# Attention's logits and values as full-array products, the other head's half filled with zeros

## The chip, the core and the metric

The kernel runs on one core of one Trainium2 chip. The metric is the device time of one execution in microseconds (us), the median of several runs; less is better. TensorE (PE) does the matrix products and has a row of its own for its weight loads (PEld); VectorE (DVE), ScalarE (ACT) and GpSimd (POOL) do the rest, and SyncE (SP) issues the transfers.

## The reference

Two transformer blocks over 256 tokens of width 1024, in float32. Block 1 adds a mixer of three branches and an MLP; block 2 has two layers, each a mixer and an MLP. What matters here are the attentions, 40 heads of width 64 in all:

- block 1: 8 query heads over 2 key heads, on the 64 keys per query that an index score picks (4 index heads of width 64), with a learned bias;
- block 2, layer 0: 8 heads with forget gates and 8 heads with a relative bias;
- block 2, layer 1: 8 stick-breaking heads and 8 latent heads, whose queries and keys have 96 rows (64 plain, 32 rotary).

```python
s = jnp.einsum('bqhd,bkhd->bhqk', qb, k).astype(jnp.float32) * scale   # logits
...
p = jax.nn.softmax(jnp.where(mask, s, -jnp.inf), axis=-1)
return jnp.einsum('bhqk,bkhd->bqhd', p.astype(v.dtype), v)             # values
```

Around them stand dense products with weights: 1024 to some 6,700 columns in block 1's mixer, 1024 to 4096 and back in each of the three MLPs.

## The kernel before

Activations lie transposed: features on the 128 partitions, the 256 tokens along the free axis, in K tiles of 128 features. All weights are one stream of 128 by 128 blocks in the order of use. A unit of eight blocks is split into two parts, `whi` on ACT (L168) and `wlo` on DVE (L170), five units in flight of each. A dense product takes three products of parts per block: L225, L228, L229 where features stay on partitions, L264 (`gemm_tokens`) where tokens come out on partitions, as the attention's values do; L237 and L238 are the wide form of the MLP's second product.

Attention is side work. `pipeline` is a generator over the heads; `slot`, called after each dense tile, runs its next step, and the step's instructions are put among the dense ones. A planner that simulates the engines in time settles the order on each queue. A step has the logits of one head (`scores`, L409 and L416) with its softmax (L427 to L433), the transposes of an earlier head's weights (`transpose_p`, L439), and the values product of the head before that (`pv`, L446 and L447), after whose second head ACT and DVE split the pair's result (`split`, L271 and L272).

Two heads share a 128-row tile: head g of a pair lies in rows 64g to 64g+63 of `qT` and `kT`. Logits of one head are taken from those 64 rows alone, a 64 by 128 form of the array; in block 1 and layer 0 the second query block goes in three products of parts (`kh`, `kl`, `qh`, `ql`). Values of one head take 64 columns of the values as the loaded operand, a 128 by 64 form, and write 64 partitions of the bank `po`; the pair's other head writes the other 64. Latent heads take 96 rows. Three small products use few rows: index weights (L535, 4 rows), the forget gates' sums per query (L877, 8 rows) and per key (L914, 40 rows). A float32 product stands in the trace as two matmul records, a product of parts as one.

The queries come from L898 (layer 0) and L990 (layer 1), one DVE instruction of 128 by 256 that applies the norm's scale; the values from `gemm_tokens`, evicted by ACT at L267. The linear attention's products at L722 use 32 and 64 columns, and its last products, L743 and L744, are float32 of 128 by 128 with the same moving widths as L446 and L447.

Of the kernel before, what the change touches and what calls it, by code (L numbers as in the profile page):

```python
# [18 lines left out]
T = 256  # L19
# [56 lines left out]
def kernel(  # L76
# [47 lines left out]
    # the first products want the first K tiles of both operands  # L124
# [11 lines left out]
    nc.vector.memset(eps, EPS)  # L136
    ident = cst[:, C_ID:C_ID + 128]
# [83 lines left out]
    def gemm(ps, ks, ah, al, prev=None):  # L221
        """ps = W.T @ a over the K tiles ks; three of the four products of the parts."""
# [9 lines left out]
    def gemm_wide(kt, a):  # L232
        """[128, 2, T] of which the halves' sum is W.T @ a, both parts of a[:, k] at once."""
# [22 lines left out]
    def gemm_tokens(kt, ah, al, dst, scale=None, steps=1):  # L256
        """dst(b) [128, 256] = (a.T @ W)[128 * b:] for 256 columns of W, times scale[:, b]: tokens on partitions."""
# [8 lines left out]
        for b, ps in enumerate(banks):  # L266
            nc.scalar.activation(out=dst(b), in_=ps, func=AF.Copy, scale=1.0 if scale is None else scale[:, b:b + 1])  # L267
# [6 lines left out]
    def rsqrt(src, n, inv_n, dst, room=None):  # L274
        """dst = (src * inv_n + EPS) ** -0.5 over [128, n]: exp(-ln/2) and a Newton step."""
# [8 lines left out]
    def softplus_neg_abs(dst, z):  # L284
        """dst = ln(1 + exp(-|z|))"""
# [4 lines left out]
    def sigmoid(dst, z, t):  # L290
        """dst = exp(min(z, 0) - ln(1 + exp(-|z|)))"""
# [5 lines left out]
    def operand(j, gain):  # L297
        """Operand parts of x[:, j] * gain."""
# [6 lines left out]
    def squares(j):  # L305
        """The squares of x[:, j] on top of those before."""
# [22 lines left out]
    def rstd_tokens():  # L329
        """rtok[t, b] = rstd of token 128 * b + t"""  # L330
# [20 lines left out]
    def mlp(gain_next):  # L351
# [6 lines left out]
        with ExitStack() as st:  # L358
# [11 lines left out]
            for j in range(KD):  # L370
                # the sum of the parts costs a step, which the last tile does without
# [5 lines left out]
                # the last tile of all goes on in halves of the tokens  # L377
# [18 lines left out]
    def v_natural(dst, vT, rows):  # L396
        """dst[:, kt, :] = vT[:, kt * 128:].T"""
        ps = pt_p.tile([128, 512], FP32, name="pt")
        n = rows.stop - rows.start
        for kt in range(2):  # L400
            nc.tensor.transpose(out=ps[:, kt * n:(kt + 1) * n], in_=vT[rows, kt * 128:(kt + 1) * 128],
                                identity=ident[rows, rows])
        src = ps[:, 0:2 * n].rearrange("p (k c) -> p k c", k=2)
        nc.scalar.activation(out=dst, in_=src, func=AF.Copy)

    def scores(qT, kT, rows, parts=None):
# [37 lines left out]
    def pv(po, pT, v, cols):  # L444
        """po [64, 256] = (P @ v).T: keys 0..127 for all queries, keys 128..255 for queries 128..255."""
        m = nc.tensor.matmul(out=po, lhsT=v[:, 0, cols], rhs=pT[:, 0:256], start=True, stop=False)  # L446
        after(nc.tensor.matmul(out=po[:, 128:256], lhsT=v[:, 1, cols], rhs=pT[:, 256:384], start=False, stop=True), m)  # L447

    class Pair:
        """Two heads whose outputs fill one K tile of the next product: probs(g) gives [128, 384] of weights,  # L450
        v the values, oh and ol the parts to fill."""
# [11 lines left out]
        def s3(self, g):  # L463
            if g == 0:
                self.po = po_p.tile([128, 512], FP32, name="po")[:, 0:T]
            v = self.v() if callable(self.v) else self.v
            pv(self.po[g * HD:(g + 1) * HD], self.pT.pop(g), v, slice(g * HD, (g + 1) * HD))
# [7 lines left out]
    def pipeline(pairs, d):  # L475
        """The heads of the pairs one step apart: logits and softmax, d steps later transposes, then values."""
# [14 lines left out]
    # ================= block 1 =================  # L491
# [16 lines left out]
    with ExitStack() as st:  # L508
# [13 lines left out]
        # -- sparse attention: index queries and keys, then keys, values and queries --  # L522
        ps = gemm1(KD, xh, xl)
        ikT = att.tile([128, T], FP32, name="ikT")
        nc.vector.tensor_tensor(out=ikT[0:64], in0=ps[0:64], in1=rstd[0:64], op=ALU.mult)
        nc.vector.tensor_tensor(out=ikT[64:128], in0=ps[0:64], in1=rstd[0:64], op=ALU.mult)
        iwT = att.tile([128, 384], FP32, name="ir", bufs=2)[:, 0:T]
        nc.vector.scalar_tensor_tensor(out=iwT[64:68], in0=ps[64:68], scalar=1.0 / 16.0, in1=rstd[64:68],
                                       op0=ALU.mult, op1=ALU.mult)
        iw = att.tile([128, 2, 4], FP32, name="iw")  # L530

        def index_weights():
            ps = pt_p.tile([128, 512], FP32, name="pt")
            for b in range(2):
                nc.tensor.transpose(out=ps[:, b * 4:b * 4 + 4], in_=iwT[64:68, b * 128:(b + 1) * 128],  # L535
                                    identity=ident[64:68, 64:68])
# [11 lines left out]
        vn = att.tile([128, 2, 128], FP32, name="vn")  # L548

        def select():  # L550
            """Index scores (block 0 in columns 0..127, block 1 in 128..383) and what they leave out."""
            for h in range(4):
                rows = slice(64 * (h % 2), 64 * (h % 2) + 64)
                ps = scores(iqT[:, h // 2], ikT, rows)
# [734 lines left out]
```

## Time and profile before

| | us |
|---|---|
| median of 3 runs | 1100.3 (1099.16 to 1103.56) |
| span of the profiled execution | 1098.2 |
| PE busy | 1078.4 (98%) |
| DVE busy | 833.4 (76%) |
| ACT busy | 600.9 (55%) |
| POOL busy | 151.2 (14%) |

The profile is of one execution on the one core; its granted TensorE clock was full nearly throughout (mean 0.998). In time order the span holds: block 1's mixer to about 290 us (attention's index scores from 20, its heads from 77 to 123, linear attention to 200, gates and output to 290), MLP to 468, layer 0's mixer to 610 (attention 485 to 605), MLP to 786, layer 1's mixer to 918 (attention 798 to 910), MLP and last norm to 1098. A matmul's record lasts from its start to the modelled end of its pipeline, so records overlap; how fast PE works is read from start to start.

### The profile page before, as it was taken

What the parts mean: (1) busy time and instruction counts of PE and PEld (TensorE: products, weight loads), DVE (VectorE), ACT (ScalarE), POOL (GpSimd) and SP (SyncE); (2) the same over time, 40 slices, a digit from 0 to 9 for tenths busy, and PEclk for the clock granted to TensorE, in tenths of its full rate; (3) what the DMA queues carried; (4) which work ended last, traced back from release to release, by engine and by line L of the source; (5) the groups of instructions that cost most, each with busy time, mean ns of one, the idle gap of its engine ahead of it and who ended that gap; (6) DMA issues with size and microseconds to landing.
All of it is one profiled execution on the core that took longest, in us unless ns stands there. A gap on an engine that the chain in (4) does not pass through costs nothing. (4 is left out here: it accounts for less than half of the span.)

```text
span 1098.2 us, 20294 instructions
## 1 busy us (share of the span) xinstructions
PE 1078.4 (98%) x8132; PEld 1008.0 (92%) x8132; DVE 833.4 (76%) x1606; ACT 600.9 (55%) x943; POOL 151.2 (14%) x164
## 2 busy tenths in 40 slices
PE   7999999999999999999999999999999999999996
PEld 6998989999999988998888999988999889999886
DVE  7999798887986666687667866666689679776663
ACT  6467456665565544455554555444458655555441
POOL 1035450110300001110001200011021004000110
PEclk9999999999999999999999999999999999999999
DMA  8543333454455554563333545455454323555541
GB/s 308 201 164 135 127 144 132 181 192 155 169 216 192 192 179 179 184 226 116 116 116 116 191 179 181 182 189 192 154 192 154 116 93 142 209 195 195 186 174 39
DMA packets 29007, 183.94 MB, mean 167 GB/s; under 512 B 3056, under 2 KB 6384, under 8 KB 7280
## 3 DMA queue, kind: packets, MB, share of 16 engines
q1 hardware_dynamic: 28768, 182.50, 45.7%
q8 instruction: 64, 1.05, 0.4%
q14 instruction: 31, 0.25, 0.1%
q10 hardware_dynamic: 144, 0.13, 0.0%
HBM read 181.57 MB, written 1.05 MB: 166 GB/s over the span
## 5 line engine op out<-in xcount | busy, mean ns | idle before, releaser
L170 DVE TENSOR_TENSOR wlo<-stg,whi 128x512 fp32r<-128x512 f32 (+1 forms) x676 | 473.3, 741 | 164.9 <-ACT whi L168 160.8
L168 ACT ACTIVATE whi<-stg 128x1024 fp32r<-128x1024 f32 (+1 forms) x340 | 356.2, 1051 | 343.7 <-PE pg L228 195.7
L225 PE MATMUL pg<-xh,whi 128*128 128x256 f32 x1472 | 416.0, 283 | 7.2 <-ACT whi L168 6.8
L229 PE MATMUL pg<-xh,wlo 128*128 128x256 f32 x1472 | 414.1, 282 | 0.6 <-DVE wlo L170 0.6
L228 PE MATMUL pg<-xl,whi 128*128 128x256 f32 x1472 | 413.3, 281 | 0.6 <-DVE xl L300 0.6
L225 PEld LDWEIGHTS pg<-xh,whi 128*128 128x128 f32 x1472 | 277.4, 189 | 12.6 <-ACT whi L168 7.1
L229 PEld LDWEIGHTS pg<-xh,wlo 128*128 128x128 f32 x1472 | 279.4, 190 | 2.7 <-DVE wlo L170 1.3
L228 PEld LDWEIGHTS pg<-xl,whi 128*128 128x128 f32 x1472 | 277.9, 189 | 3.3 <-issue 1.2
L237 PE MATMUL pg<-hid,whi 128*128 128x512 f32 x672 | 236.1, 396 | 0.0
L238 PE MATMUL pg<-hid,wlo 128*128 128x256 f32 x672 | 188.5, 281 | 0.0
L237 PEld LDWEIGHTS pg<-hid,whi 128*128 128x128 f32 x672 | 126.1, 188 | 30.1
L238 PEld LDWEIGHTS pg<-hid,wlo 128*128 128x128 f32 x672 | 127.0, 189 | 0.0
L308 POOL TENSOR_TENSOR sqa<-xv 128x256 f32<-128x256 f32 x6 | 4.3, 720 | 480.3 <-DVE xv L384 300.1
L312 POOL TENSOR_TENSOR sq<-xv 128x256 f32<-128x256 f32 x36 | 27.7, 776 | 175.6 <-DVE xv L384 171.7
L429 ACT ACTIVATE p<-p,m 128x128 f32<-128x128 f32 x64 | 28.5, 446 | 23.1 <-DVE m L427 22.8
L228 PE MATMUL pg<-ol,whi 128*128 128x256 f32 x128 | 37.1, 292 | 0.0
L264 PE MATMUL pg<-whi,xh 128*128 128x256 f32 x128 | 37.1, 290 | 0.0
L313 POOL TENSOR_TENSOR sqa<-sqa,sq 128x256 f32<-128x256 f32 x36 | 36.7, 1019 | 2.4
L225 PE MATMUL pg<-oh,whi 128*128 128x256 f32 x128 | 36.0, 291 | 0.5 <-ACT oh L271 0.5
L229 PE MATMUL pg<-oh,wlo 128*128 128x256 f32 x128 | 36.2, 285 | 0.0
L369 DVE TENSOR_TENSOR hid<-s,hid 128x512 fp32r<-128x512 f32 x48 | 33.1, 690 | 4.0
L264 PE MATMUL pg<-wlo,xh 128*128 128x256 f32 x128 | 35.9, 281 | 0.0
(344 smaller groups left out, 1565.1 us busy)
## 6 DMA issues: line engine op xcount, KB each, us to landing
stg<-w SPq DMA_DIRECT2D x168, 1024.0 KB, 4.8
t<-t_bias SPq DMA_DIRECT2D x8, 128.0 KB, 2.8
cb<-chk_bias SPq DMA_DIRECT2D x1, 1024.0 KB, 4.7
xv<-x_in SPq DMA_DIRECT2D x2, 384.0 KB, 6.1
cst<-consts SPq DMA_DIRECT2D x1, 640.0 KB, 10.9
stg<-w SPq DMA_DIRECT2D x1, 512.0 KB, 7.8
out<-xg SPq DMA_DIRECT2D x2, 256.0 KB, 2.5
stg<-w SPq DMA_DIRECT2D x1, 384.0 KB, 6.5
```

Source lines behind the costliest of these rows:

```text
L168: act = [nc.scalar.activation(out=h[:, z], in_=src[:, z], func=AF.Copy) for z in (pieces if u == 0 else [slice(0, UW)])]
L170: dve = [nc.vector.tensor_tensor(out=l[:, z], in0=src[:, z], in1=h[:, z], op=ALU.subtract) for z in pieces]
L225: m0 = nc.tensor.matmul(out=ps, lhsT=h, rhs=ah[:, k], start=(k == ks[0]), stop=False)
L228: nc.tensor.matmul(out=ps, lhsT=h, rhs=al[:, k], start=False, stop=False)
L229: m1 = nc.tensor.matmul(out=ps, lhsT=l, rhs=ah[:, k], start=False, stop=(k == ks[-1]))
L237: nc.tensor.matmul(out=ps, lhsT=h, rhs=a[:, k], start=(k == 0), stop=False)
L238: nc.tensor.matmul(out=ps[:, 1], lhsT=l, rhs=a[:, k, 0], start=False, stop=(k == kt - 1))
L264: nc.tensor.matmul(out=ps, lhsT=a[:, k, t], rhs=w_, start=(k == 0 and i == 0), stop=(k == kt - 1 and i == 2))
L312: nc.gpsimd.tensor_tensor(out=s, in0=x[:, j], in1=x[:, j], op=ALU.mult)
L313: nc.gpsimd.tensor_tensor(out=sqa, in0=sqa, in1=s, op=ALU.add)
L369: nc.vector.tensor_tensor(out=hid[:, j:j + 2, 1], in0=s, in1=hid[:, j:j + 2, 0], op=ALU.subtract)
L429: nc.scalar.activation(out=p[:, a:b], in_=p[:, a:b], func=AF.Exp, scale=-1.0, bias=m[:, i:i + 1], accum_out=sums[:, i:i + 1])
```

## The change

Every product of attention takes all 128 rows and all 128 columns of the array. Where two heads share a tile, one operand gets a copy per head, `[128, 2, ...]`, in which the other head's 64 rows are zero, so a product over 128 rows gives one head's logits. For block 1 that operand is the keys (`ikT`, `kz` and its parts), for the other two the queries (`qT`, `qh`, `ql`), made by one DVE instruction of twice the width against a scale `rq` that is zero in the other half. Values stand in a tile with 64 zero columns after each head's 64 (`values_room`, zeroed once by POOL), so that 128 columns taken at the right place hold one head's values in its half and zeros in the other; both heads of a pair then add into all of `po`, as one group of four products. The 4-, 8- and 40-row products get 128 rows. Latent heads' logits keep 96 rows, and L722 is not touched. To make room, some tiles share buffers: `isc` takes one of the three of `p`, `bm` those of `ir`, `kz` that of `ikT`, and the squares and scales of the two latents one each.

The diff, cut to its core (the same edits recur where "..." stands):

```diff
+    half = keep.tile([128, 2], FP32, name="half")
+    nc.gpsimd.memset(half, 0.0)
+    for g in range(2):
+        nc.gpsimd.memset(half[64 * g:64 * g + 64, g:g + 1], HD ** -0.5)
...
+    def values_room(name, heads):
+        v = att.tile([128, 2, heads, 128], FP32, name=name)
+        nc.gpsimd.memset(v[:, :, :, 64:128], 0.0)
+        return v
+    def head_values(v, h):
+        o = 128 * h - 64 * (h % 2)
+        return [v[:, kt].rearrange("p h c -> p (h c)")[:, o:o + 128] for kt in range(2)]
...
-        nc.tensor.matmul(out=ps[:, 0:128], lhsT=qT[rows, 0:128], rhs=kT[rows, 0:128], start=True, stop=True)
+        nc.tensor.matmul(out=ps[:, 0:128], lhsT=qT[:, 0:128], rhs=kT[:, 0:128], start=True, stop=True)
...
-            nc.tensor.matmul(out=ps[:, 128:384], lhsT=q[rows], rhs=k[rows, 0:256], start=(i == 0), stop=(i == len(terms) - 1))
+            nc.tensor.matmul(out=ps[:, 128:384], lhsT=q, rhs=k[:, 0:256], start=(i == 0), stop=(i == len(terms) - 1))
...
+    def query_scale(name):
+        r = att.tile([128, 2, T], FP32, name=name)
+        for g in range(2):
+            nc.vector.tensor_scalar(out=r[:, g], in0=rstd, scalar1=half[:, g:g + 1], scalar2=None, op0=ALU.mult)
+        return r
...
-    def pv(po, pT, v, cols):
-        m = nc.tensor.matmul(out=po, lhsT=v[:, 0, cols], rhs=pT[:, 0:256], start=True, stop=False)
-        after(nc.tensor.matmul(out=po[:, 128:256], lhsT=v[:, 1, cols], rhs=pT[:, 256:384], start=False, stop=True), m)
+    def pv(po, pT, v, g):
+        m = nc.tensor.matmul(out=po, lhsT=v[0], rhs=pT[:, 0:256], start=(g == 0), stop=False)
+        after(nc.tensor.matmul(out=po[:, 128:256], lhsT=v[1], rhs=pT[:, 256:384], start=False, stop=(g == 1)), m)
...
-            pv(self.po[g * HD:(g + 1) * HD], self.pT.pop(g), v, slice(g * HD, (g + 1) * HD))
+            pv(self.po, self.pT.pop(g), self.v(g), g)
...
+        ikT = att.tile([128, 2, T], FP32, name="ikT")
+        nc.gpsimd.memset(ikT[64:128, 0], 0.0)
+        nc.gpsimd.memset(ikT[0:64, 1], 0.0)
...
-        isc = att.tile([128, 384], FP32, name="isc")
+        isc = att.tile([128, 384], FP32, name="p", bufs=pb["p"])
...
+                made["kz"] = kz = att.tile([128, 2, T], FP32, name="ikT")
+                for g in range(2):
+                    nc.vector.scalar_tensor_tensor(out=kz[:, g], in0=raw[:, 0], scalar=gk[:, g:g + 1], in1=rr[:, 0:T],
+                                                   op0=ALU.mult, op1=ALU.mult)
...
-                bm = att.tile([128, 384], FP32, name="bm", bufs=2)
+                bm = att.tile([128, 384], FP32, name="ir", bufs=2)
...
-                    made["k"] = tuple(att.tile([128, T], FP32R, name=n) for n in ("kh", "kl"))
-                    split(*made["k"], raw[:, 0])
+                    made["k"] = tuple(att.tile([128, 2, T], FP32R, name=n) for n in ("kh", "kl"))
+                    split(*made["k"], made["kz"])
...
-                nc.tensor.transpose(out=ps[:, b * 8:b * 8 + 8], in_=fc[0:8, b * 128:(b + 1) * 128],
-                                    identity=ident[0:8, 0:8])
+                nc.tensor.matmul(out=ps[:, b * 8:b * 8 + 8], lhsT=fc[:, b * 128:(b + 1) * 128], rhs=ident[:, 0:8],
+                                 start=True, stop=True)
...
+        rq = query_scale("rq")
+        vz = values_room("vz", 16)
         def qk(name):
-            qT = att.tile([128, T], FP32, name="qT", bufs=4)
+            qT = att.tile([128, 2, T], FP32, name="qT", bufs=4)
...
-            nc.vector.scalar_tensor_tensor(out=qT, in0=gemm1(KD, xh, xl), scalar=HD ** -0.5, in1=rstd,
-                                           op0=ALU.mult, op1=ALU.mult)
+            nc.vector.tensor_tensor(out=qT, in0=_mid(gemm1(KD, xh, xl), 2), in1=rq, op=ALU.mult)
...
-            split(qh, ql, qT[:, 128:256])
+            split(qh, ql, qT[:, :, 128:256])
...
-                    nc.tensor.matmul(out=pc, lhsT=row[:, h:h + 1].to_broadcast([40, 128]), rhs=fparts,
+                    nc.tensor.matmul(out=pc, lhsT=row[:, h:h + 1].to_broadcast([128, 128]), rhs=fparts,
...
-            gemm_tokens(KD, xh, xl, lambda b: vn[:, b], rtok)
+            gemm_tokens(KD, xh, xl, lambda b: vz[:, b, 2 * j:2 * j + 4, 0:64], rtok)
...
-            sq = att.tile([128, n, T], FP32, name=f"{name}_sq")
-            rs = att.tile([128, T], FP32, name=f"{name}_rs")
+            sq = att.tile([128, n, T], FP32, name="l_sq")
+            rs = att.tile([128, T], FP32, name="l_rs")
...
-        vm = att.tile([128, 2, 4, 128], FP32, name="vm")
+        vm = values_room("vm", 8)
+        vs = values_room("vs", 8)
+        rq = query_scale("rq")
```

## Rows read from the trace of the kernel before

**Rows 1.** The page: busy time (share of the span) and instructions of each engine.

```profile
PE 1078.4 (98%) x8132; PEld 1008.0 (92%) x8132; DVE 833.4 (76%) x1606; ACT 600.9 (55%) x943; POOL 151.2 (14%) x164
```

**Rows 2.** Stretches from:to, length, then busy us (instructions) by engine, clock, DMA.

```profile
20.00:60.00 40.00, 40.00 (x323) 37.85 (x323) 37.80 (x107) 21.05 (x26) 3.18 (x3) 1.00 0.54 201
60.00:125.00 65.00, 65.00 (x503) 58.98 (x502) 57.70 (x135) 38.53 (x83) 25.41 (x27) 1.00 0.41 149
485.00:605.00 120.00, 119.57 (x875) 105.19 (x874) 84.16 (x249) 63.17 (x145) 5.35 (x7) 1.00 0.35 125
798.00:910.00 112.00, 111.53 (x829) 99.16 (x828) 91.59 (x214) 73.58 (x154) 18.86 (x29) 1.00 0.38 139
```

**Rows 3.** Timeline of PE, layer 1: start us, duration us, engine, line, form; 64-row logits.

```profile
799.03 0.28 PE L225 MATMUL pg<-xh,whi 128*128 128x256 f32 x1
799.24 0.48 PE L409 MATMUL sc<-kT,qT 64*128 64x128 f32 x2
...
800.43 0.28 PE L225 MATMUL pg<-xh,whi 128*128 128x256 f32 x1
```

**Rows 4.** The same view, 96-row logits of a latent head.

```profile
847.63 0.28 PE L229 MATMUL pg<-xh,wlo 128*128 128x256 f32 x1
847.74 0.39 PE L409 MATMUL sc<-km,qm 96*128 96x128 f32 x2
...
848.64 0.28 PE L229 MATMUL pg<-xh,wlo 128*128 128x256 f32 x1
```

**Rows 5.** The same view, layer 0, one head's values in the 64-column form.

```profile
592.25 0.28 PE L225 MATMUL pg<-oh,whi 128*128 128x256 f32 x1
592.46 0.65 PE L446 MATMUL po<-pT,vn 128*64 128x256 f32 x2
...
593.59 0.28 PE L225 MATMUL pg<-oh,whi 128*128 128x256 f32 x1
```

**Rows 6.** The same view, linear attention's values, 128 by 128.

```profile
183.41 0.28 PE L228 MATMUL pg<-xl,whi 128*128 128x256 f32 x1
183.53 0.59 PE L743 MATMUL po<-A,inat 128*128 128x256 f32 x2
...
184.42 0.28 PE L228 MATMUL pg<-xl,whi 128*128 128x256 f32 x1
```

**Rows 7.** The same view, one 40-row product of parts alone.

```profile
492.85 0.28 PE L228 MATMUL pg<-xl,whi 128*128 128x256 f32 x1
493.06 0.38 PE L914 MATMUL sc<-fparts,row 40*128 40x256 f32 x1
...
493.71 0.28 PE L228 MATMUL pg<-xl,whi 128*128 128x256 f32 x1
```

**Rows 8.** The same view: the first and the last visit to a partial form.

```profile
23.10 0.28 PE L535 MATMUL pt<-cst,ir 4*128 4x4 f32 x2
...
903.68 0.65 PE L446 MATMUL po<-pT,vm 128*64 128x256 f32 x2
```

**Rows 9.** The same view, block 1, two heads' logits between one another.

```profile
85.38 0.28 PE L229 MATMUL pg<-xh,wlo 128*128 128x256 f32 x1
85.59 0.59 PE L409 MATMUL sc<-raw 64*128 64x128 f32 x3
...
86.92 0.28 PE L229 MATMUL pg<-xh,wlo 128*128 128x256 f32 x1
```

**Rows 10.** Groups of instructions: busy us, mean ns | idle before, releasers.

```profile
L898 DVE SCALAR_TENSOR_TENSOR qT<-pg,rstd 128x256 f32<-128x256 f32 x8 | 3.3, 419 | 1.8 <-PE pg L229 1.5
L798 DVE TENSOR_TENSOR gz<-pg,rstd 128x512 f32<-128x512 f32 x12 | 8.2, 686 | 3.4 <-PE pg L229 3.2
L168 ACT ACTIVATE whi<-stg 128x1024 fp32r<-128x1024 f32 (+1 forms) x340 | 356.2, 1051 | 343.7 <-PE pg L228 195.7 <-PE pg L237 106.8 <-issue 29.4
```

**Rows 11.** Stretches of two MLPs, columns as in rows 2.

```profile
640.00:690.00 50.00, 50.00 (x426) 50.00 (x426) 34.92 (x54) 28.27 (x37) 0.00 (x0) 1.00 0.52 189
950.00:1000.00 50.00, 50.00 (x440) 49.90 (x439) 34.91 (x54) 30.02 (x37) 0.00 (x0) 1.00 0.55 200
```

More of the change, by code (lines that the diff above doesn't have):

```diff
@@ L266, in gemm_tokens @@
         for b, ps in enumerate(banks):
-            nc.scalar.activation(out=dst(b), in_=ps, func=AF.Copy, scale=1.0 if scale is None else scale[:, b:b + 1])
+            o = dst(b)
+            nc.scalar.activation(out=o, in_=ps.rearrange("p (h c) -> p h c", h=o.shape[1]), func=AF.Copy,
+                                 scale=1.0 if scale is None else scale[:, b:b + 1])
         slot(2 * kt / KD * steps)
@@ L393, in mlp, with v_natural, scores @@
                     nc.scalar.activation(out=xg[:, j], in_=x[:, j], func=AF.Copy, scale=v_("norm_final", j))
-    def v_natural(dst, vT, rows):
+    def values_room(name, heads):
[5 more added lines that the diff above has]
+        return [v[:, kt].rearrange("p h c -> p (h c)")[:, o:o + 128] for kt in range(2)]
+    def v_natural(dst, vT):
         ps = pt_p.tile([128, 512], FP32, name="pt")
-        n = rows.stop - rows.start
         for kt in range(2):
[L401 to L406, printed above, removed]
+            nc.tensor.transpose(out=ps[:, kt * 128:(kt + 1) * 128], in_=vT[:, kt * 128:(kt + 1) * 128], identity=ident)
+        for kt in range(2):
+            nc.scalar.activation(out=dst[:, kt, :, 0:64], func=AF.Copy,
+                                 in_=ps[:, kt * 128:(kt + 1) * 128].rearrange("p (h c) -> p h c", h=2))
+    def scores(qT, kT, parts=None):
         ps = sc_p.tile([128, 512], FP32, name="sc")
-        nc.tensor.matmul(out=ps[:, 0:128], lhsT=qT[rows, 0:128], rhs=kT[rows, 0:128], start=True, stop=True)
+        nc.tensor.matmul(out=ps[:, 0:128], lhsT=qT[:, 0:128], rhs=kT[:, 0:128], start=True, stop=True)
         if parts:
@@ L534, in index_weights @@
             for b in range(2):
[L535 to L536 removed]
+                nc.tensor.matmul(out=ps[:, b * 4:b * 4 + 4], lhsT=iwT[:, b * 128:(b + 1) * 128], rhs=ident[:, 64:68],
+                                 start=True, stop=True)
             nc.vector.tensor_copy(out=iw, in_=ps[:, 0:8].rearrange("p (b h) -> p b h", b=2))
@@ L543 @@
             scaled(iqT[:, j], gemm1(KD, xh, xl))
-        isc = att.tile([128, 384], FP32, name="isc")
+        isc = att.tile([128, 384], FP32, name="p", bufs=pb["p"])
         selm = att.tile([128, 384], FP32, name="selm")
         raw = att.tile([128, 5, T], FP32, name="raw")
-        vn = att.tile([128, 2, 128], FP32, name="vn")
+        vn = values_room("vn", 2)
+        gk = att.tile([128, 2], FP32, name="gk")
+        nc.gpsimd.memset(gk, 0.0)
+        for g in range(2):
+            nc.vector.tensor_copy(out=gk[64 * g:64 * g + 64, g:g + 1], in_=v_("k_norm_g")[64 * g:64 * g + 64])
         def select():
             for h in range(4):
-                rows = slice(64 * (h % 2), 64 * (h % 2) + 64)
-                ps = scores(iqT[:, h // 2], ikT, rows)
+                ps = scores(iqT[:, h // 2], ikT[:, h % 2])
                 r = att.tile([128, 384], FP32, name="ir", bufs=2)
@@ L588, in unit_heads @@
             rsqrt(ps[:, 0:n].rearrange("p n t -> p (n t)"), n * T, 1.0 / HD, rr[:, 0:n * T])
-            nc.vector.scalar_tensor_tensor(
-                out=raw[:, j0:j0 + n].rearrange("p n t -> p (n t)"),
-                in0=raw[:, j0:j0 + n].rearrange("p n t -> p (n t)"), scalar=(gq if j0 else v_("k_norm_g")),
-                in1=rr[:, 0:n * T], op0=ALU.mult, op1=ALU.mult)
+            if j0 == 0:
+                made["kz"] = kz = att.tile([128, 2, T], FP32, name="ikT")
+                for g in range(2):
+                    nc.vector.scalar_tensor_tensor(out=kz[:, g], in0=raw[:, 0], scalar=gk[:, g:g + 1], in1=rr[:, 0:T],
+                                                   op0=ALU.mult, op1=ALU.mult)
+            else:
+                q = raw[:, j0:j0 + n].rearrange("p n t -> p (n t)")
+                nc.vector.scalar_tensor_tensor(out=q, in0=q, scalar=gq, in1=rr[:, 0:n * T], op0=ALU.mult, op1=ALU.mult)
             yield
@@ L643 @@
         scaled(vT, gemm1(KD, xh, xl))
-        later(lambda: v_natural(vn, vT, slice(0, 128)))
+        later(lambda: v_natural(vn, vT))
         for j in range(5):
@@ L987, in qk @@
         def qk(name):
-            qT = att.tile([128, T], FP32, name="qT", bufs=3)
+            qT = att.tile([128, 2, T], FP32, name="qT", bufs=3)
             kT = att.tile([128, T], FP32, name="kT", bufs=3)
-            nc.vector.scalar_tensor_tensor(out=qT, in0=gemm1(KD, xh, xl, rate[0]), scalar=HD ** -0.5, in1=rstd,
-                                           op0=ALU.mult, op1=ALU.mult)
+            nc.vector.tensor_tensor(out=qT, in0=_mid(gemm1(KD, xh, xl, rate[0]), 2), in1=rq, op=ALU.mult)
             scaled(kT, gemm1(KD, xh, xl, rate[0]))
@@ L996, in values @@
         def values(i):
-            made[f"v{i}"] = vn = att.tile([128, 2, 256], FP32, name="vn", bufs=2)
-            gemm_tokens(KD, xh, xl, lambda b: vn[:, b], rtok, rate[0])
+            gemm_tokens(KD, xh, xl, lambda b: vs[:, b, 4 * i:4 * i + 4, 0:64], rtok, rate[0])
         def stick(j, slot_):
```

45 lines of the change are left out of this document (21 added, 24 removed).

## The prediction

> **What bounds the kernel now.** I read the page's busy table first, then the busy time by stretches of the four places where attention's products lie, then the timeline of PE around single visits of those products, and last the costs on the other engines. The busy table [rows 1] has PE at 98% and DVE at 76%; that alone says little, since a matmul's record overlaps the next. The stretches [rows 2] say more: in block 1 PE is busy for 40.00 of 40 and 65.00 of 65 us, in layer 0 for 119.57 of 120, in layer 1 for 111.53 of 112. So PE never waits long for weights or for a softmax, and a time saved on PE's own queue is a time saved, as long as the others follow. ACT, which starts the split of each weight unit, has 343.7 us of idle time before those splits and 302.5 of them end with a matmul of PE [rows 10]: it waits for PE to give buffers back, so the weights run ahead.
>
> Then the steps from start to start in the timeline. Dense products follow each other in about 0.118 us. Around attention's products something else is lost:
>
> - A stick-breaking head's logits, 64 rows: from the last dense product before them to the third after them it is 799.03 to 800.43, 1.40 us [rows 3].
> - A latent head's logits, 96 rows, with the same number of records and the same widths: 847.63 to 848.64, 1.01 us [rows 4]. So 0.39 us goes with the 64-row form, not with the float32 product or with its place among dense ones.
> - One head's values, 64 columns: 592.25 to 593.59, 1.34 us [rows 5]. The linear attention's values, same widths with 128 columns: 183.41 to 184.42, 1.01 us [rows 6]. Here 0.33.
> - One 40-row product of parts alone: 492.85 to 493.71, 0.86 us [rows 7], where four dense steps would take 4 x 0.118 = 0.47. Again 0.39, so the kind of number makes no difference.
>
> **The change, part by part.** *What it removes.* A visit to a partial form loses time on the way in and on the way back. Into 64 rows and back to full both come with a load of 128 columns, so I split 0.39 evenly, 0.195 each; into 64 columns then is 0.33 - 0.195 = 0.135. I went through PE's matmuls in order of time, from the first visit to the last [rows 8], and counted each change of form outside L722, which keeps its own: 51 into few rows, 41 into 64 columns, 78 back to full (in 14 places one partial form follows another), 75 visits. The sum is 51 x 0.195 + 41 x 0.135 + 78 x 0.195 = 30.7 us. By stretch [rows 2]: 2.0 us in 20 to 60 (5 in, 5 back), 5.8 in 60 to 125 (10 and 8 in, 14 back), 14.8 in 485 to 605 (28 and 17 in, 36 back), 8.2 in 798 to 910 (8 and 16 in, 23 back).
>
> *What it adds on PE.* Moving widths and the number of records stay. Values load 128 columns in place of 64; the group of rows 6 does that with the same moving widths, and its 1.01 us equals that of the 96-row group, so the longer load hides behind the moving columns. Adding both heads into one bank is the same four products in the same order, and the split still follows the second head. Nothing, then.
>
> *What it gives up.* In four places the two heads' 64-row products run side by side. In the clearest one both heads' logits take 85.38 to 86.92, 1.54 us [rows 9]; one after the other they are three dense steps (0.35), four float32 records of 128 columns at 0.11 (the group of rows 4 less three dense steps, 0.66 us over 768 columns) and six products of parts at 0.118, 1.50 us, and 0.39 for the visit, 1.89. So 0.35 us was saved there, and for the four together I take 1.0 us as the bound. The Trainium skill, "TensorEngine Tiling (Array Packing)", section "Tiling Modes", speaks against the change: smaller tiles of the array work independently, and a contraction of 64 rows or fewer could go up to twice as fast. By that rule filling the array would throw half its rate away; the trace has it in 4 places only.
>
> *What it adds on DVE.* Queries of 128 by 512 in place of 128 by 256: 686 against 419 ns [rows 10], 0.27 us for each of 12, 3.2 us. The lower parts of eight query tiles double, at most 0.27 each, 2.1. Four `rq` instructions, two copies for `gk`, and a second `kz` and a wider split of it are at most 0.42 each, 3.4. In all at most 8.7 us: 5.0 in layer 0, 1.9 in layer 1, 1.7 in block 1 (rounded). The same step on ACT (wider `qh`, two evictions for `v_natural`) is less. Shares after it, from rows 2: layer 0 (84.2 + 5.0) / (120 - 14.8) = 85%, layer 1 (91.6 + 1.9) / (112 - 8.2) = 90%, block 1 from 20 to 125 (95.5 + 1.7) / (105 - 7.8) = 100%. In the layers PE covers it and I cost it at nothing; in block 1 that cover is used up. Weights run ahead there, and the stage ends only after linear attention, so I charge 1.0 us of the 7.8 and keep all 7.8 as the bound.
>
> *Waits it adds.* ACT's first value eviction waits for POOL's zeros, and weight splits are queued behind it. In layer 0 five dense tiles come before it, 5 x 24 x 0.118 = 14 us, and POOL is busy for 5.35 of 120 us [rows 2]: nothing, unless POOL is held up by more than those 14 us. The second latent's first square on POOL waits for the first latent's sums on PE, since the squares share a buffer; at that rate [rows 4] those 1,536 columns are an estimated 1.3 us, behind it is queued the next square, and its reader comes a tile later: nothing. `kz` waits for the last index logits, some 25 us earlier; `isc` leaves its buffer before the heads want it. SP's queue gets no transfer more. For the ends of the two layers, where the last pair's values, their split and the last dense group follow one another, I charge 0.3 us.
>
> **Sum.** -30.7 + 1.0 + 1.0 + 0.3 = -28.4 us. The profiled span is 1098.2, so 1069.8; the median lies 2.1 above that span, and with the same 2.1 it is 1071.9. I predict 1072 us.
>
> **The rivals.**
>
> *DVE becomes the bound.* For it: 95% busy in 20 to 60, and the 100% above. Against it: ACT's idle time before the splits, and a PE that waits for nothing in the same stretches now. If block 1 keeps none of its 7.8 us and layer 1 half of its 8.2, the gain is 28.4 + 1.0 - 7.8 - 4.1 = 17.5 us: 1083.
>
> *The dense pace falls another way.* The second MLP runs 426 products in 50 us, the third 440 [rows 11], 0.1174 and 0.1136 us each, for the whole stage; the first runs as the second. The profile doesn't show what sets it; in the mixers it changes after single visits. A different stream before an MLP may turn it. Over the 768 products of an MLP's first half that is 2.9 us, and at most as much again in the second half; I take 4.4. Both slow ones turned fast: 1072 - 8.8 = 1063. The fast one turned slow: 1076. This is width, not another outcome.
>
> *Side by side.* If two heads' logits ran in parallel wherever they could, the change would cost 20 pairs x 0.35 = 7 us in place of the 1.0: 1078. The trace bears it out in 4 places, so it gets a small chance. This is the rule of the Trainium skill named above ("TensorEngine Tiling (Array Packing)", "Tiling Modes").
>
> *Slower: the lost time is not the form's.* If something else about these visits makes the gap, such as the scattered order or the semaphores at their ends, then it stays, and the wider DVE work comes on top: between 1.7 us (block 1, where DVE is full) and 8.7 us, 1102 to 1109. It decides at 8.7 / 75 visits, 0.12 us: a visit that gets less than that back makes the kernel slower. Against it stand two groups in full form, as scattered as the others, that lose nothing [rows 4, 6], and a single 40-row product that loses as much as a whole group [rows 7]. The change not doing what it says (a planner that spreads the products over more places) ends near the same, since in full form a visit costs nothing wherever it lies.
>
> **How the numbers follow.** The forecast with its pace variants 0.73, DVE as the bound 0.15, side by side 0.05, a gain that is mostly lost in ways not listed, within 0.5% of 1100.3 (about what a measurement of this kernel can tell from no change), 0.04, slower 0.03. The range reaches from 1063 (both paces fast) to 1084 (DVE as the bound). Faster by over 0.5% then is 0.73 + 0.15 + 0.05 = 0.93, within 0.04, slower 0.03.
>
> **What would show it.** In the timeline of PE a head's logits and values should read 128*128, and the three-product step around them should be near 1.0 us, not 1.3 to 1.4; only L722 should keep a partial form. The stretch of layer 0's attention should shrink by some 14 us, layer 1's by 8, block 1's by 5 to 8. If DVE binds, PE gets idle time ended by `wlo` in block 1. If the MLPs' spans change, it is the pace. Wrong would be a full-form visit that still loses 0.2 us or more, or PE waiting for a softmax in the layers.

## The result, and the profile after

| | before | changed |
|---|---|---|
| time, median of 4 runs each | 1100.2 us | 1085.3 us (1084.8 to 1085.9) |
| ratio, 95% interval | | 0.9866 (0.9849 to 0.9884) |
| profiled span | 1098.2 us | 1084.1 us |
| matmul records | 8132 | 8136 |

The change is faster by 1.3%, 14.9 us, where 28 were forecast; the time lies just outside the range. The busy table of the page hides where the rest went, as the one of [rows 1] did:

```profile
PE 1061.3 (98%) x8136; PEld 1022.7 (94%) x8136; DVE 838.4 (77%) x1613; ACT 601.7 (56%) x944; POOL 156.2 (14%) x174
```

PE is as full as before; its weight loads are busy for 14.7 us longer in a shorter span, which was the first hint at what follows. Now the timeline of PE in the changed kernel, columns as in [rows 3]: the single product of parts and a head's values in layer 0, and a stick-breaking head's logits in layer 1.

```profile
489.67 0.28 PE L230 MATMUL pg<-xh,whi 128*128 128x256 f32 x1
489.79 0.28 PE L949 MATMUL sc<-fparts,row 128*128 128x256 f32 x1
489.91 0.38 PE L428 MATMUL sc<-kT,qT 128*128 128x128 f32 x2
...
576.15 0.28 PE L233 MATMUL pg<-ol,whi 128*128 128x256 f32 x1
576.26 0.59 PE L472 MATMUL po<-pT,vz 128*128 128x256 f32 x2
...
577.16 0.29 PE L233 MATMUL pg<-ol,whi 128*128 128x256 f32 x1
...
787.78 0.28 PE L234 MATMUL pg<-xh,wlo 128*128 128x256 f32 x1
787.90 0.38 PE L428 MATMUL sc<-kT,qT 128*128 128x128 f32 x2
...
788.79 0.28 PE L234 MATMUL pg<-xh,wlo 128*128 128x256 f32 x1
```

From the last dense product ahead of the group to the third behind it the logits take 1.01 us (1.40 in [rows 3]), the values 1.01 (1.34 in [rows 5]), and the single product is one dense step of 0.12, where in [rows 7] the visit took 0.39 us beyond its dense steps. So the visits became what the forecast said. Yet the stretches of the changed kernel that answer to [rows 2] (shorter than those, so that each holds about the same work):

```profile
20.00:60.00 40.00, 40.00 (x329) 39.64 (x328) 39.26 (x111) 22.11 (x29) 2.81 (x3) 1.00 0.56 202
60.00:123.00 63.00, 63.00 (x520) 62.29 (x519) 58.19 (x135) 39.56 (x84) 30.91 (x28) 1.00 0.43 153
484.00:594.00 110.00, 109.57 (x902) 108.47 (x902) 89.28 (x256) 65.40 (x148) 7.30 (x9) 1.00 0.42 146
782.00:887.00 105.00, 104.48 (x817) 101.57 (x816) 90.48 (x213) 70.82 (x147) 12.67 (x24) 1.00 0.40 141
```

VectorE is busy for 98% of the first stretch. There PE gets 6 products further than before, where the forecast's 2.0 us are some 17.

I then went through PE's stream product by product, took from each step the one that a product of its width needs undisturbed, and added up what was left: steps next to a partial form; steps next to other small products; steps over 121 ns between dense products (waits); and the rest, the pace. In us, before and after: partial forms 33.5 and 3.4 (30.1 gone, 30.7 forecast); other small products 4.5 and 8.2; waits 7.9 and 11.5; pace -6.4 and +1.4. So some 15 of the 30.1 came back: 7.8 through the pace of the dense products, 7.3 through waits and the steps next to other small products. By stage, from its first dense product to the next stage's first, told by the operands' names (an MLP is 768 products of `xh` and `xl` and those of `hid` behind them; half alone and half 512 are experiments below):

| us | before | changed | half alone, e1 | half 512, e3 |
|---|---|---|---|---|
| block 1 | 280.3 | 281.0 | 284.5 | 277.7 |
| first MLP | 183.3 | 182.2 | 182.5 | 184.0 |
| layer 0 | 134.4 | 121.6 | 135.6 | 120.2 |
| second MLP | 183.5 | 182.7 | 183.3 | 183.5 |
| layer 1 | 123.0 | 117.7 | 124.5 | 116.7 |
| third MLP | 178.9 | 183.5 | 183.5 | 183.4 |

By these bounds the mixers of the kernel before end at 285, 603 and 909 us, some us ahead of the times given with its profile. Several expectations below have stage times by other bounds (281.8 for block 1 in e3, say); what they compare is answered by this table. Each column is one profile.

Block 1 lost all its gain and more, and the third MLP, which the change doesn't touch, grew by 4.6 us. The dense steps themselves had changed: 2,041 steps of 113 or 114 ns before and 13 after, and 2,299 of 120 ns after, some 680 before.

### The profile page after: what moved, and what is told of

Its sections match the earlier page's. It is cut to its first block, busy times and chain, and to the rows that moved or that the text cites. A ratio compares the mean times of both kernels' runs of the same rounds, so it can differ in the third digit from the quotient of the medians.

```text
span 1084.1 us, 20315 instructions
## 1 busy us (share of the span) xinstructions
PE 1061.3 (98%) x8136; PEld 1022.7 (94%) x8136; DVE 838.4 (77%) x1613; ACT 601.7 (56%) x944; POOL 156.2 (14%) x174
## 4 chain that ended last, share of the span: by engine, by line
PE 90%; DVE 6%; issue 1%; ACT 1%; DMA 1%; POOL 0%; SPq 0%; DVEq 0%; POOLq 0%
PE pg L233 19%; PE pg L234 19%; PE pg L230 19%; PE pg L242 14%; PE pg L243 7%; PE pg L269 4%; DVE wlo L175 3%; PE sc L435 2%; PE po L472 2%; PE pt L465 1%; PE sc L428 1%; PE po L473 1%; DVE xl L307 1%; DMA stg<-w 1%; ACT whi L173 1%
## 5 line engine op out<-in xcount | busy, mean ns | idle before, releaser
L242 PE MATMUL pg<-hid,whi 128*128 128x512 f32 x672 | 233.1, 391 | 0.0
L269 PE MATMUL pg<-whi,xl 128*128 128x256 f32 x128 | 36.6, 286 | 0.0
```

Source lines behind the costliest of these rows:

```text
L242: nc.tensor.matmul(out=ps, lhsT=h, rhs=a[:, k], start=(k == 0), stop=False)
L269: nc.tensor.matmul(out=ps, lhsT=a[:, k, t], rhs=w_, start=(k == 0 and i == 0), stop=(k == kt - 1 and i == 2))
```

## The experiments

**The added tile.** The diff puts `half`, 8 bytes a partition, into the first pool. All that is allocated behind it moves by 32 bytes, the weights' parts `whi` from address 76800 to 76832 and `wlo` from 97280 to 97312 among it, while the operand's parts `xh` and `xl` stay. Theory 1: the place sets the pace. Theory 2: the visits to partial forms did, by where they interrupted PE. e1 is the kernel before with `half` alone; e2 and e3 give the changed kernel a longer `half`.

```diff
# e1, kernel before
+    half = keep.tile([128, 2], FP32, name="half")
+    nc.gpsimd.memset(half, 0.0)
+    for g in range(2):
+        nc.gpsimd.memset(half[64 * g:64 * g + 64, g:g + 1], HD ** -0.5)
# e2 [128, 16], e3 [128, 128], e4 [128, 32], e9 [128, 48]; changed kernel
-    half = keep.tile([128, 2], FP32, name="half")
+    half = keep.tile([128, 16], FP32, name="half")
```

> The kernel before with one thing of the change alone: the tile half, 8 bytes a partition, and its three memsets on POOL. It moves every tile allocated behind it by 32 bytes: the parts of the weights from 76800 and 97280 (multiples of 512) to 76832 and 97312, the MLP's hidden operand from 128000 to 128032. Theory 1, the place of the operands: the dense products lose their 113.3 ns pace for 117 to 120 ns, as in the changed kernel, and the time is 1105 to 1110 us (1100.2 + the 7.8 us of lost pace, more or less). Theory 2, the pace is set by the visits of small products: those are all still there, so the pace stays at 113.3 and 117.8 ns and the time at 1100 +- 1 us.

> The changed kernel with half made 64 bytes long instead of 8, so that the weights and the hidden operand begin at multiples of 64 (76864, 128064) and not at multiples of 64 plus 32. Theory 1, the place of the operands, if 64 bytes is the step that counts: the 113.3 ns pace is back and the time is 1075 to 1079 us (1085.3 less the 7.8 us of pace, and the stalls as they are). If a longer step counts: 1085. Theory 2, the visits set the pace: 1085 +- 1 us and a pace of 117 to 120 ns as in the changed kernel.

> The changed kernel with half made 512 bytes long, so that every tile behind it stands modulo 512 where it stood in the kernel before. Theory 1, the place of the operands, whatever the step up to 512: 1075 to 1079 us and a pace with 113.3 ns in it. Theory 2, the visits set the pace: 1085 +- 1 us, pace 117 to 120 ns.

Measured: e1 1110.1 us, 1.0092 of before (1.0061 to 1.0123): an unused tile of 8 bytes costs 10 us, 6.9 of them in the three mixers by the table. e2 1087.8; e3 1081.1, 0.9823 (0.9767 to 0.9880), less than the changed kernel's 1085.3, but short of the 1075 to 1079 that I expected. Theory 2 is out. The stretch 210 to 240 us has nothing but dense products; it shows the pace as the number of products (columns as in [rows 2]), here in the kernel before, in e1 and in e3:

```profile
210.00:240.00 30.00, 30.00 (x263) 30.00 (x262) 25.13 (x35) 20.69 (x27) 7.53 (x4) 1.00 0.53 189
```

```profile
210.00:240.00 30.00, 30.00 (x256) 30.00 (x255) 25.33 (x36) 20.10 (x26) 7.52 (x4) 1.00 0.53 190
```

```profile
210.00:240.00 30.00, 30.00 (x262) 30.00 (x261) 24.48 (x34) 20.79 (x28) 5.83 (x4) 1.00 0.53 192
```

263, 256, 262; the changed kernel has 256, e2 255. 64 bytes were not enough, 512 were.

**Which place: the weights', the operand's, or the distance?** e4 and e9 move the weights further. e5 moves `xh` and `xl` to a multiple of 512 and leaves the weights as in e3; e8 moves the weights after them.

```diff
# e5 and e8, changed kernel; half is [128, 112] in e5, [128, 128] in e8
+    room0 = keep.tile([128, 16], FP32, name="room0")
+    nc.gpsimd.memset(room0, 0.0)
     xh = keep.tile([128, KD, T], FP32R, name="xh")
```

> The changed kernel with half made 128 bytes long: the parts of the weights and the hidden operand begin at multiples of 128, but 128 behind a multiple of 512 (64 behind one did not bring the pace back, 0 did). If the step that counts is 128 bytes: the 113.3 ns pace in the mixer stages as with half of 512 bytes, 1080 to 1082 us. If it is 256 or 512: pace 117 to 120 ns, 1085 to 1088 us.

> The changed kernel with half of 512 bytes, and 64 bytes put ahead of the operand's parts xh and xl as well (taken off half again), so that they too begin at a multiple of 512 and not 64 short of one; weights as in the run with 512 bytes. Theory 1a, only the place of the weights' parts counts: 1081 +- 1.5 us, 113 ns in the mixers' products as before. Theory 1b, each operand's own place counts: more of the mixers' products at 113 ns or under it, 2 to 5 us less, 1076 to 1079. Theory 1c, the distance of the two operands modulo 512 counts (64 was good; 96 and 128 were bad; now 0): the pace goes somewhere else altogether, to 117 to 120 ns (1085 to 1088) if 64 was a lucky one.

> The changed kernel with 64 bytes ahead of xh and half of 512 bytes: against the run that moved xh and xl alone by 64 bytes (1094.2 us, a pace of 120 ns), the weights' parts move by 64 too. xh and xl begin at a multiple of 512, the weights 64 behind one: each stands where it was bad (xh at 0: 1094; weights at 64 behind: 1087.8), but the distance of the two modulo 512 is 64 again, as in the kernel before and in the run at 1081.1. If the distance of the two operands counts: 1080 to 1083 us with 113.3 ns in the mixers. If each one's own place counts: 1087 to 1095 us, pace 119 to 120 ns.

> The changed kernel with half of 192 bytes: the weights' parts stand 256 bytes from the operand's parts modulo 512, the farthest there is. Distances so far, and time: 0, 1094.2; 64, 1081.1; 96, 1085.3; 128, 1087.8; 192, 1080.6. If the two operands' reads get in each other's way where they are close, the farthest is the best: a pace of 113 to 118 ns, 1076 to 1080 us. If there is no such order: 1085 to 1088.

Measured, with the distance of the weights from `xh` modulo 256 bytes and the products in 210 to 240 us:

| run | distance | products | time, us |
|---|---|---|---|
| before; e3; e8 | 64 | 263; 262; 262 | 1100.2; 1081.1; 1081.7 |
| changed; e1 | 96 | 256; 256 | 1085.3; 1110.1 |
| e2 | 128 | 255 | 1087.8 |
| e4 | 192 | 256 | 1080.6 |
| e5; e9 | 0 | 252; 252 | 1094.2; 1093.9 |

The same stretch in e5 and in e8:

```profile
210.00:240.00 30.00, 30.00 (x252) 30.00 (x251) 25.23 (x33) 20.21 (x27) 6.31 (x4) 1.00 0.50 178
```

```profile
210.00:240.00 30.00, 30.00 (x262) 30.00 (x261) 24.48 (x34) 20.35 (x27) 6.69 (x4) 1.00 0.55 202
```

e5 put both operands on the roundest addresses and lost 13 us; e8 has each where it was bad alone, and only the distance right, and has it all back. So the distance counts. e9 was to be the best, "the farthest", and repeats e5 product for product: 0 and 256 are the same, the step is 256. e4 met its number, 1080 to 1082, for another reason than I gave: most of its mixers' products have not the 113 ns pace (256 products), and its MLPs' second products are 4.5 us shorter than e3's in all (89.4, 89.4 and 89.3 us against 90.9, 90.9 and 90.8). The changed kernel has the same short ones, at distance 96; why stays unexplained.

**VectorE in block 1.** From 120 to 170 us of e3 VectorE (third pair of numbers) has 0.08 us free of 50, and PE 4.7:

```profile
120.00:170.00 50.00, 45.30 (x403) 43.29 (x403) 49.92 (x67) 28.52 (x46) 25.92 (x18) 1.00 0.35 121
```

Three of its groups from 120 to 172 us (line, operation, busy us, mean ns) are the splits of weights and the convolution's second and third tap:

```profile
L175 DVE TENSOR_TENSOR wlo<-stg,whi 128x512 fp32r<-128x512 f32 x24 | 24.1, 1042 | 0.1
L806 DVE SCALAR_TENSOR_TENSOR uy<-u,xv,uy 128x256 f32<-128x256 f32 x3 | 4.5, 1492 | 0.0
L804 DVE SCALAR_TENSOR_TENSOR uy<-u,xv,uy 128x256 f32<-128x256 f32 x3 | 3.1, 1042 | 0.0
```

Their means hide two kinds. The same line took 0.48 us at one place and 2.16 at another, where it began just behind an operation of POOL (start us, us):

```profile
122.47 0.48 DVE L804 SCALAR_TENSOR_TENSOR uy<-u,xv,uy 128x256 f32<-128x256 f32 x1
131.40 2.16 DVE L804 SCALAR_TENSOR_TENSOR uy<-u,xv,uy 128x256 f32<-128x256 f32 x1
131.22 2.05 POOL L723 TENSOR_TENSOR dd<-G 128x1024 f32<-128x1024 f32 x1 [0.17 <-DVE mm L728]
```

Of the eight tap operations of e3 on VectorE five took 0.46 to 0.49 us and three, each begun beside `dd<-G`, 1.9 to 2.2; together they are 8.6 us, not 10.1. The splits `wlo` take 0.69 us away from POOL. By the same comparison some 13 of VectorE's 50 us here are time that its instructions take longer beside POOL, an estimate. So VectorE is full, but a quarter of it is not its own work.

e6 (on e3) and e7 (on before) move the taps' products to ScalarE, that of POOL too; e10 (on e3) and e11 (on before) leave the second and third tap out, so they compute another convolution.

```diff
# e6, e7; e10 and e11 only take the two nc.vector operations out
-    nc.gpsimd.tensor_scalar(out=y, in0=u[:, 0:T], scalar1=v_("conv_w", j * 3), scalar2=None, op0=ALU.mult)
-    nc.vector.scalar_tensor_tensor(out=y, in0=u[:, 1:T + 1], scalar=v_("conv_w", j * 3 + 1), in1=y,
-                                   op0=ALU.mult, op1=ALU.add)
-    nc.vector.scalar_tensor_tensor(out=y, in0=u[:, 2:T + 2], scalar=v_("conv_w", j * 3 + 2), in1=y,
-                                   op0=ALU.mult, op1=ALU.add)
+    taps = [y] + [hg.tile([128, T], FP32, name=n, bufs=2) for n in ("uc", "ut")]
+    for i, tap in enumerate(taps):
+        nc.scalar.activation(out=tap, in_=u[:, i:T + i], func=AF.Copy, scale=v_("conv_w", j * 3 + i))
+    nc.vector.tensor_tensor(out=y, in0=y, in1=taps[1], op=ALU.add)
+    nc.vector.tensor_tensor(out=y, in0=y, in1=taps[2], op=ALU.add)
```

> The changed kernel with half of 512 bytes, and VectorE relieved in block 1: the convolution's three taps are scaled on ScalarE (which has 40% of this stretch free), and VectorE only adds them: two additions of some 0.41 us in place of two fused ones of 1.04 and 1.49 us, four times over, 6.8 us of VectorE work less between 120 and 180 us, where it has not been idle for a moment from 125 to 170. Theory A, in block 1 VectorE is the bound once the visits are cheap (4.5 us gained by 116 us, 2.0 left at 285): the time falls by 2.5 to 5 us against the run with half of 512 bytes, 1076 to 1079, and the waits of the linear attention's products (up to 1.26 us each) shrink. Theory B, the linear attention's own chain from engine to engine sets those waits: less than 1 us, 1080 to 1082.

> The kernel before with the same relief alone: the convolution's taps on ScalarE, VectorE adds them. Theory A, VectorE is the bound only once the visits are cheap: before, the visits' gaps left it time, and only the two waits of 1.2 and 0.4 us at 153 to 159 us can go: 0.5 to 2 us, 1098 to 1100. Theory B: no more than 1 us in either kernel. If the kernel before gains as much as the changed one, VectorE bounded block 1 already, and the change took nothing off it there.

> The changed kernel with half of 512 bytes, without the second and the third tap of the convolution (their 8 fused operations on VectorE, 1.04 and 1.49 us each, 10.1 us in all, are left out; nothing is put in their place on another engine). To be read with the same cut in the kernel before. Theory A, VectorE is the bound of block 1 behind 120 us once the visits are cheap: block 1 (to 285 us) falls by 4 to 6 us against 281.8, and what the change saves in block 1, 2.0 us with the taps, is 5 to 8 us without them. Theory B, the linear attention's chain from engine to engine bounds it: falls by less than 2 us, and the change saves 2 us as before.

> The kernel before without the second and the third tap of the convolution (the same 8 operations on VectorE, 10.1 us, left out). Theory A: block 1 falls by 0 to 2 us against 283.8, since the visits' gaps in PE's stream stay and only the two waits of 1.2 and 0.4 us at 153 to 159 us can go. Theory B: less than 1 us. If it falls as much as in the changed kernel, VectorE bounded block 1 in both, and the change's gain there was never to be had.

Measured: e6 1076.9, e7 1102.8, e10 1073.2, e11 1100.6 us. Block 1 alone is read better from the first product of the MLP behind it (start us, us), in before, e3, e11 and e10:

```profile
285.29 0.28 PE L225 MATMUL pg<-xh,whi 128*128 128x256 f32 x1
```

```profile
282.52 0.28 PE L230 MATMUL pg<-xh,whi 128*128 128x256 f32 x1
```

```profile
286.43 0.28 PE L225 MATMUL pg<-xh,whi 128*128 128x256 f32 x1
```

```profile
278.86 0.28 PE L230 MATMUL pg<-xh,whi 128*128 128x256 f32 x1
```

Counted from its own first product, block 1 takes 280.3 us before and 277.7 in e3: the change saves 2.6. Without the taps it takes 281.6 and 274.0: the change saves 7.6. The same taps are worth 3.7 us behind the change, just under the 4 to 6 expected, and nothing ahead of it (e11 is even 1.3 later; I had expected 0 to 2 earlier). PE's waits from 100 to 180 us say the same: 1.9 us before, 4.8 in e3, 2.6 in e10, 2.4 in e11; 3.1 of e3's 4.8 are for VectorE. So VectorE was not the bound of block 1 before, and became it: theory A. How much of that is its own work and how much POOL's `dd<-G` beside it, no run separates. The softer relief shows less: e6's block 1 is 1.2 shorter than e3's, less than the 2.5 to 5 expected, with VectorE as busy as before; other instructions of it now stand beside `dd<-G` (one `yc_l` took 2.1 us in place of 0.4). e7's is 3.9 us longer than that of the kernel before, which neither theory had; PE waits there for the linear attention at other places, and I have not followed it further. With one profile of each, differences of about 1 us are not told from chance: e3 and e8, alike but for 64 bytes, differ by 0.9 here.

**The other operands.** The hidden operand of the MLP and the mixers' outputs stand at distance 0 from the weights in both kernels, the worst one for `xh`. e12 and e13 put 64 and 192 bytes ahead of them, e14 64 on top of e4.

```diff
# e12, e14 [128, 16]; e13, e15, e16 [128, 48]
     tmp = pool("tmp", 2)
+    gap = pool("gap").tile([128, 16], FP32, name="gap")
+    nc.gpsimd.memset(gap, 0.0)
```

> The changed kernel with half of 512 bytes, and 64 bytes put between the weights' parts and the tiles allocated behind them: the mixers' outputs and the MLP's hidden operand, until now a multiple of 256 bytes from the weights (the distance that was worst for xh: 1094 us), now stand 64 off. If the distance counts for every operand: the MLP's second product, 90.99, 86.7 and 81.12 us in the run with 512 bytes, falls by 2 to 4 us each time, and the mixers' output products by some tenths, so 1070 to 1076. If it counts only where xh is read: 1081 +- 1.5.

> The same with 192 bytes between them, so that weights less hidden operand is 64 modulo 256, as weights less xh is in the kernel before. If the distance counts for every operand, and its sign does not: as with 64 bytes, 1070 to 1076; if only this sign gives the 113.3 ns pace: this one alone is there. If it counts only where xh is read: 1081 +- 1.5.

> The changed kernel with half of 128 bytes (weights less xh is 192 modulo 256) and 64 bytes behind the weights (weights less hidden operand is 192 too). If the distance counts for every operand: 3 to 9 us under the run with half of 128 bytes alone, 1072 to 1078 us; if only for xh: 1080.6 +- 1.5.

Measured: 1075.7, 1074.3 and 1081.4 us. The two on e3 gained 5.4 and 6.8, the sum that I had expected, but not where I had expected it: the MLPs' second products went from 90.9, 90.9 and 90.8 us only to 89.7, 89.7 and 90.6 (e12) or 90.7, 90.7 and 90.6 (e13). In e13 block 1 is 1.4 shorter, layer 0 1.1, layer 1 0.6, and the second MLP's first product 2.8, which, like 3.0 in e12's third MLP, is the pace of the next paragraph. e14 gained nothing over e4 in time. The mixers' products still follow the distance. The mean step in block 1 from one dense product to the next of the same operand, in ns, steps over 121 left out:

| distance of the weights from the operand, modulo 256 | `xh`, `xl` | branch outputs `yc`, `ya`, `yh` |
|---|---|---|
| 0 | 119.7 (e5, e9) | 119.3 to 119.8 (the runs without `gap`) |
| 64 | 114.2 to 115.5 (the eleven runs there) | 113.7 to 113.8 (e13, e15, e16) |
| 96 | 117.5 (e1), 117.7 (changed) | none |
| 128 | 118.2 (e2) | none |
| 192 | 117.3 (e14), 117.5 (e4) | 117.7 (e14), 117.8 (e12) |

So 64 is the fast distance and 0 the slow one for both kinds, and the direction counts: 192, which is 64 the other way round, lies between. The MLP's second product doesn't follow it.

**The MLPs' pace.** [rows 11] had one MLP faster than another. Stretches of 45 us in the third MLP's first product: before, changed, e3, e10.

```profile
930.00:975.00 45.00, 45.00 (x400) 45.00 (x399) 33.46 (x53) 26.89 (x35) 0.00 (x0) 1.00 0.56 210
```

```profile
910.00:955.00 45.00, 45.00 (x378) 45.00 (x377) 32.25 (x51) 25.60 (x32) 0.00 (x0) 1.00 0.57 196
```

```profile
910.00:955.00 45.00, 45.00 (x385) 45.00 (x384) 31.57 (x49) 25.75 (x32) 0.00 (x0) 1.00 0.54 189
```

```profile
910.00:955.00 45.00, 45.00 (x400) 45.00 (x399) 32.49 (x51) 26.65 (x33) 0.00 (x0) 1.00 0.53 193
```

400, 378, 385, 400. At distance 64 this MLP takes 178.9 us in three profiles (before, e10, e11) and 183.4 in four (e3, e6, e7, e8), with the weights at the same distance from `xh` and `hid`; e11's second MLP is fast too, 179.0 for 183.5. Of the 4.5 us 3.0 lie in its first product (89.6 for 92.6) and 1.5 in the second. The kernel before bunches alike: its 18 runs beside e8 lie at 1094.7 to 1096.0 (2), 1099.4 to 1101.3 (13) and 1103.7 to 1104.7 (3), steps of some 4.4 us. The changed kernel (1084.8 to 1085.9), e1, e2, e4, e5 and e9 spread by 1.0 to 3.2 us in all. So at 64 each MLP falls into one of two paces, and, as the runs bunch alike, from run to run. At the other distances no first product was seen under 92 us; second products of 89.4 were (changed, e1, e2, e4). What decides in a run is open.

**All together.** e15 is e3 with the taps on ScalarE and 192 bytes ahead of the other operands; e16 is the kernel before with those 192 bytes alone.

> What helped, together: the changed kernel with half of 512 bytes, 192 bytes behind the weights' parts, and the convolution's taps scaled on ScalarE. If the parts add up: 1074.3 less the 1.9 us that the taps took off block 1, 1070 to 1074. If block 1's gain with the taps and its gain with the 192 bytes (281.8 to 279.5) are the same one: 1074 to 1076.

> The kernel before with the same 192 bytes behind the weights' parts and nothing else, so that change and no change are compared where every operand stands alike. If the 192 bytes act alike in both: 1092 to 1096 us (6 to 7 under 1100), and the change is then worth some 20 us at equal places. If they act only together with the change: 1100 +- 1.

Measured: e15 1073.4 us, 0.9713 (0.9688 to 0.9737), 12 us under the changed kernel, and the best that leaves nothing out. e16 1098.5 us, 0.9954 (0.9941 to 0.9967); its neighbours of before lay at 1104.2 this time, so it gained 5 us, not 6 to 7. In its profile the mixers are 3.2 us shorter than in the kernel before; the rest can be the MLPs' pace. At these places the change takes the profiled span from 1096.1 (e16) to 1073.4 (e13), each with one MLP in the fast pace: 22.7 us.

## Why the prediction was wrong

**The visits: right.** 30.1 us of steps next to partial forms went, 30.7 forecast; layer 0 at equal places lost 14.2 (134.4 to 120.2) of 14.8. What is left, 3.4 us, is the form that L722 keeps (L755 in the changed kernel). The counts of the prediction make 78 visits and not 75, which moves only the time per visit that decides for slower, to 0.11 us. The Trainium skill, "TensorEngine Tiling (Array Packing)", section "Tiling Modes", says that a change of mode drains TensorE; the trace agrees, at 0.39 us for a visit to 64 rows. By the same section's rule on independent tiles (the factor of two that the prediction gives with it stands in the page's "Overview") the change would have lost 7 us; layer 0 shows no such loss.

**The failed step: the place of the tiles counted as nothing.** The sum has terms for what the change adds on PE, on DVE and in waits, and none for `half` and its 8 bytes, or for any tile that comes to lie elsewhere. It listed the MLPs' pace as width that "A different stream before an MLP may turn"; that "in the mixers it changes after single visits" it noted and priced at nothing. The pace hangs on the distance that `half` changed: the tile costs 10.1 us in the kernel before (e1) and 4.2 in the changed one (e3 against 1085.3). Of the 7.8 us of lost pace 3.7 are the distance's directly (pace -2.3 in e3, +1.4 in the changed kernel), and the rest the third MLP's, which has two paces at 64.

**Block 1: the charge was mis-sized.** "I charge 1.0 us of the 7.8 and keep all 7.8 as the bound": with the taps the change saves 2.6, without them 7.6, so VectorE took 5.0, POOL's part in it included. The rows were there: 57.70 of 65 us, and 95% in 20 to 60 [rows 2]. I read the share of 20 to 125 and not of the stretch behind it, 125 to 170, where the linear attention fills it: 44.52 of 45 us in the kernel before, with PE still at 43.06. That stretch had no room for a PE that comes sooner:

```profile
125.00:170.00 45.00, 43.06 (x383) 41.39 (x383) 44.52 (x62) 25.94 (x42) 25.89 (x18) 1.00 0.33 118
```

The rival with VectorE as the bound had the mechanism for block 1, though not its sign: PE's waits there end with the linear attention's `A` and `mm`, not with `wlo`. That its 1083 lies near the 1085.3 measured is luck, since it has nothing of the tiles' place. The 1.0 us charged for heads that ran side by side is not told apart from the rest of block 1.

**Layer 1: 6.3 of 8.2 at equal places.** Waits there grew from 1.5 to 3.6 us. VectorE's 91.33 of 105 us in e3 (87%) is near the 90% that I took for cover; from 801 to 835 us, where the latents are made, it is 33.50 of 34, and PE waits in that stretch:

```profile
801.00:835.00 34.00, 33.35 (x263) 32.10 (x262) 33.50 (x73) 27.06 (x57) 5.32 (x7) 1.00 0.43 156
```

But VectorE was nearly as full in the stretch of the kernel before that answers to it, 31.19 of 32, with no wait of PE:

```profile
818.00:850.00 32.00, 32.00 (x252) 30.04 (x251) 31.19 (x68) 25.13 (x52) 5.59 (x7) 1.00 0.44 163
```

And PE's 0.6 us of waits in e3's stretch end with ACT (its `vm` and `qm`), not with VectorE. What took the 1.9 us of layer 1 stays open.

**The sum at equal places.** Block 1 2.6, layer 0 14.2, layer 1 6.3, together 23.1 us from before to e3, and 22.7 of span from e16 to e13 (2.0, 14.8 and 6.2 in the same stages). The forecast of 28 was some 5 too high: 3 in block 1, where VectorE is the bound, and 2 in layer 1. The 8 from there to the 14.9 measured went with the place of the tiles: 5.7 in the mixers (3.3, 1.4 and 1.0 between changed and e3) and 2.7 in the MLPs, where the third fell into the slow pace and lost 4.6.

## What to carry to other kernels

Before a change's arithmetic, look at what it allocates: a few bytes ahead of the big tiles can cost as much as the change brings, so compare addresses of old and new kernel, and try a padded one. When PE's queue is shortened, ask for each other engine's share in stretches of some tens of microseconds behind the saving, not in the mean of a stage: 91% from 20 to 125 us [rows 2] was 99% in the 45 us behind. See there too whether its instructions take longer than elsewhere: a full engine may be waiting for another. Where runs of one kernel bunch at fixed steps, compare stages of profiles, not single times.

## What the runs showed of the hardware

- Dense products of parts, 128 by 128 by 256, run at some 113.3, 117 to 118 or 120 ns each, in the mixers by where the weights lie from the moving operand modulo 256 bytes: of 0, 64, 96, 128 and 192, 64 is best (262 products in 30 us), 0 worst (252). The granted clock was 0.995 to 0.998 in every profile, so it is no matter of the clock. Why is open. The Trainium skill, "SBUF — State Buffer", section "Who interferes with whom", gives TensorE separate read ports for the moving operand and for weight loads and says that it never waits on anyone. The section is on engines that work beside one another; taken for TensorE's own two reads as well, it would leave the addresses without effect, and here they have one.
- An MLP has two paces at distance 64, 4.5 us apart.
- A fused multiply and add over 128 by 256 took VectorE 0.46 to 0.49 us, and 1.9 to 2.2 where it began beside POOL's `dd<-G` of some 2 us (e3: five and three of eight). Its tile is read 4 or 8 bytes off its start in both kinds, so the offset is not what costs.
